# Wide products and compressed-block products cut into units of one weight tile and interleaved

## The chip, the cores and the metric

The kernel runs on one core of a Trainium2 chip. The metric is the device time of one execution in microseconds, here called us. Inside the core, PE (TensorE) multiplies matrices, PEld is its weight load, DVE (VectorE) and ACT (ScalarE) work element by element, POOL is GpSimd, and SP (SyncE) issues most of the transfers (DMAs).

## The reference

A decoder trunk of two layers over 1024 tokens of width 1024, in fp32. Layer A mixes tokens with a gated short convolution, layer B with sparse attention whose keys and values come in three kinds (compressed blocks, selected blocks, a sliding window). Both layers also attend to 256 memory tokens and end with a squared-ReLU MLP. What matters here, cut:

```python
for layer in range(2):
    h = rmsnorm(x, mix_norm[layer])
    mkv = mem_h @ mem_w_kv[layer]               # keys and values of the 256 memory tokens
    if layer == 0:
        z = h @ a_w_in[0]; y_tok = short_conv_mixer(z[..., :2304], a_conv_w[0])
    else:
        z = h @ b_w_in[0]                       # 768 queries, 36 gates, 256 memory queries
        y_tok = nsa_mixer(z[..., :768], z[..., 768:804], b_q_gain[0], *shared, rel_bias)
    y_mem = memory_attention(q_mem, mkv, ...)   # 4 heads
    x = x + concatenate([y_tok, y_mem]) @ w_out[layer]
    x = x + square(relu(rmsnorm(x, mlp_norm[layer]) @ w_up[layer])) @ w_down[layer]
    if layer == 0:
        kv = rmsnorm(x, kv_norm) @ w_kv_shared  # six parts of 128 columns
        # compress: overlapping blocks of 32 tokens, flattened to 2048, twice (keys, values)
        kc, vc = [gelu((blocks(kv, i) + cmp_pos[i]) @ cmp_w1[i]) @ cmp_w2[i] for i in (0, 1)]
        shared = (kc, vc, ks, vs, kw, vw)
```

## The kernel before

Tokens are worked in two chunks of 512 (c is 0 or 1). Every fp32 operand is split into a high and a low part (H and L), and a product is three matmuls: H with H, H with L, L with H (lines 265 to 267).

All weights are streamed from HBM in the order of a list called `plan`. An entry is a unit: a function and the weight tiles that it eats, each of at most 128x512 floats (256 KB). For a tile, `w_dma` (line 276) issues the load into `wraw` from SP; ACT writes its high part `wH` (line 261); DVE writes the low part `wL` (line 262). There are three buffers each of `wraw`, `wH` and `wL` (WB is 3), so a fourth load waits until the first tile's subtraction on DVE is done. `w_get` splits up to three tiles ahead and asks for two loads more.

Most units are dense: weights are stationary, 512 tokens are the moving columns, one output tile of 128 channels takes 24 matmuls and two weight tiles. Two other kinds stand among them:

- `wide`: tokens on partitions, weights as the moving operand, 8 k-steps into up to four PSUM banks (`mm,mm,lgb,lgb`). It makes the memory keys and values (`memkv_unit`, weights `mkv_w`, 512 columns, two banks), the keys and values of layer B (K, `kvt_w`, 512), the gates with the memory queries (M, `bm_w`, 292), and the queries in two groups of 384 (Q and q, `bq_w`). Each of these is one unit of 8 weight tiles. Its result goes through `heads`: copies and squares on ACT, sums on DVE, a power on POOL, transposes on PE (line 602), a scaled copy `hn` on ACT (line 606, one buffer) and a store (line 611).
- `cmp_unit`: the first product of the compression (line 1237, 256 columns, weights `cw1`, called cw in rows). One unit is two weight tiles with 8 matmuls, four units for the keys (c in ORDER) and four for the values (d) of each chunk.

ORDER (line 28) gives the sequence of these groups for each chunk, with u and U for the two dense units that feed the compression. P2 and P3 (lines 29 and 30) say how many dense units `weave` (line 1448) puts ahead of each group. The second layer's memory unit stands in `plan` after the convolution units of chunk 0 (line 1522), ahead of the output products. When a layer-B stage's groups are done, `attention` starts: its loads (ks, vs, kw, vw by POOL, T by SP) run beside the dense units that follow.

An issue planner with estimated costs lets evacuations run as threads beside the units; the recorded instructions are then ordered per engine, and loads may be put forward.

Of the kernel before, what the change touches and what calls it, by code (L numbers as in the profile page):

```python
# [24 lines left out]
S, D = 1024, 1024  # L25


ORDER = 'uUKccccMddddqQ', 'uUKccccMddddQq'
P2 = [0, 0, 1, 0, 5, 1, 2, 2, 2, 1, 1, 2, 0, 1]
P3 = [8, 0, 0, 0, 0, 1, 1, 0, 1, 0, 1, 1, 0, 4]  # L30
NTAIL = 6
AHEAD = 1
PACE = 2.5
# [4 lines left out]
KT = D // 128  # L38
# [25 lines left out]
class Issue:  # L64
# [30 lines left out]
    def spawn(self, gen):  # L95
        th = [gen, 0.0, False]
        self.threads.append(th)
        return th
# [32 lines left out]
def mmc(n):  # L131

    return (n if n >= 256 else 4 * n) / 2400
# [11 lines left out]
def trunk(ctx: ExitStack, tc: tile.TileContext, a, out):  # L145
# [11 lines left out]
    V, ACT, POOL, PE, DMA, LD = nc.vector, nc.scalar, nc.gpsimd, nc.tensor, nc.sync, nc.gpsimd  # L157
# [31 lines left out]
    qd = [[scratch(f"qd{c}_{t}", [128, 2, CH]) for t in range(6)] for c in range(2)]  # L189
# [14 lines left out]
    iss = Issue()  # L204
    chain, spawn = iss.chain, iss.spawn
# [140 lines left out]
    R, Hs = {}, {}  # L346
# [184 lines left out]

    FOUR = (mm, mm, lgb, lgb)

    def wide(hs, cols, evac, n, banks):

        kp = 512 // cols
        ps = []
        for b in banks:
            ps.append((yield from b.get())[:, :cols])
        for k in range(KT):  # L540
            if k % kp == 0:
                H, L = yield from w_get(n + k // kp, cols)
            yield lambda: len(hs) > k
            yield hs[k][2]
            for j in range(len(ps)):
                xH, xL = (x[:, 128 * j:128 * j + 128] for x in hs[k][:2])
                three(ps[j], xH, xL, H[:, k % kp], L[:, k % kp], k == 0, k == KT - 1)
                iss.pe(3 * mmc(cols))
                yield 0
        spawn(evac(ps, banks))  # L550

    def heads(ps, banks, nh, gains, dsts, dones, more=None, rkey=None):

# [58 lines left out]
            dones[i].t = max(t, t1) + 2.5  # L612
        raws.put(len(rw))

    def memkv_unit(l, dones, n):
        def evac(ps, banks):
            done = dones[2]

            def more(j):
                t = v_rows(ps[j][:, 256:], mvd[l][128 * j:128 * j + 128])  # L620
                done.t = t + 2.5
                return t
            yield from heads(ps, banks, 4, [nmkg[:, l:l + 1]] * 2, mkd[l], dones, more)
        yield from wide(Hs["mem"], 512, evac, n, (mm, lgb))


    def finish(pv, parts, dst, done):
# [422 lines left out]
            return free  # L1050
        yield from dense(n, Hs["a", c], evac)

    def qmem_wide(dones, n):
        yield from wide(Hs["a", 1], 256, lambda ps, banks: heads(
            ps, banks, 4, [mqg[:, 0:1]] * 2, mqd[0][1], dones, None, (0, 1)), n, FOUR)

    def first_units(*ns):

# [93 lines left out]
            return done.t  # L1152
        yield from dense(n, Hs["kv", c], evac)

    def kv_unit(c, dones, n):
# [9 lines left out]
        yield from wide(Hs["kv", c], 512, evac, n, FOUR)  # L1165

    def q_unit(c, i, dones, n):
        yield from wide(Hs["b", c], 384, lambda ps, banks: heads(
            ps, banks, 6, [qg] * 3, [qd[c][3 * i + t] for t in range(3)], dones), n, FOUR)

    def memgate_unit(c, dones, n):
# [15 lines left out]
        yield from wide(Hs["b", c], 292, evac, n, FOUR)  # L1187


    FS = {}  # L1190
# [31 lines left out]
    hid, through = {}, set()  # L1222

    def cmp_unit(kvi, c, j, flag, n):
        m = 64 + 2 * (31 + c)
        yield lambda: (kvi, c) in FS
        FT, t = FS[kvi, c]
        yield t
        if j == 0:
            hid[kvi, c] = yield from pvb.get()  # L1230
        ps = hid[kvi, c]
        for k in range(4):
            kk = 4 * j + k
            if k % 2 == 0:
                H, L = yield from w_get(n + k // 2, 256)
            for i, x in enumerate((H, L)):
                PE.matmul(ps[:m, :256], FT[kk // 8][:, kk % 8, :m], x[:, k % 2],
                          start=(kk == 0 and i == 0), stop=(kk == 15 and i == 1))
# [84 lines left out]
    def unit(lst, fn, *args, w=()):  # L1323
        lst.append((fn, args, w))
# [21 lines left out]
    def conv_units(m, c, t):  # L1346
        w = a["a_w"]
        unit(m, a_gate_c, c, t, w=[w[2 + 3 * t]])
        unit(m, a_u, c, t, w=[w[3 + 3 * t]])
        unit(m, a_gate_b, c, t, w=[w[4 + 3 * t]])  # L1350
# [44 lines left out]
                unit(m, down_unit, c, t, last, w=[a["wd"][l, b, t]])  # L1395
        return m

    def memkv_units(l, flags):
        m = []
        fl = [Flag(), Flag(), Flag()]  # L1400
        flags += fl
        unit(m, memkv_unit, l, fl, w=[(a["mkv_w"][l], 512)])
        return m

    normed = set()

    def b_norm(c):
# [6 lines left out]
    def kvb_units(c, flags):  # L1414
        m = []
        w = a["kv_w"]
        us = [Flag(), Flag()]

        def flag():
            flags.append(Flag())  # L1420
            return flags[-1]

        fl = [flag(), flag()]
        js = [0, 0]
        for ch in ORDER[c]:
            g = []
            if ch in "uU":
                i = "uU".index(ch)
                unit(g, u_unit, i, c, us[i], w=[w[i]])
                start(g, cmp_start, i, c, us[i])  # L1430
            elif ch == "K":
                unit(g, kv_unit, c, [flag(), flag(), flag()], w=[(a["kvt_w"], 512)])
            elif ch in "cd":
                i = "cd".index(ch)
                unit(g, cmp_unit, i, c, js[i], fl[i], w=[a["cw1"][i, js[i]]])
                js[i] += 1
            elif ch == "M":
                unit(g, memgate_unit, c, [flag(), flag(), flag()], w=[(a["bm_w"], 292)])
            else:
                i = "Qq".index(ch)  # L1440
                unit(g, q_unit, c, i, [flag(), flag(), flag()], w=[(a["bq_w"][i], 384)])
            m.append(g)
            if len(m) == 3:
# [57 lines left out]
    conv_units(plan, 0, 1)  # L1501
    plan += memkv_units(0, fmk[0])
    start(plan, mem_attn, 0, 0, fmq[0] + fmk[0], fy[0])
    for t in range(2, 6):
        conv_units(plan, 0, t)

    def after(n, box):

# [23 lines left out]
    plan += m[-8:]  # L1532


    unit(plan, qmem_wide, fmq[1], w=[(a["am_w"], 512)])
    start(plan, mem_attn, 0, 1, fmq[1] + fmk[0], fy[1])
    fkv, fat = {0: [], 1: []}, {0: [], 1: []}

# [166 lines left out]
```

## Time and profile before

| what | us |
|---|---|
| median of 3 runs | 2446.8 (2444.61 to 2448.54) |
| profiled execution, whole | 2446.22 |
| its span, first to last instruction | 2444.4 |
| PE busy | 2409.7 |
| DVE busy | 1509.3 |
| ACT busy | 1286.2 |

The granted clock over the span is 0.999. The profile names for each engine the time it was busy; for a gap it names the instruction that ended it. A matmul's record lasts longer than the distance at which the next may start, so busy PE time hides the short gaps: the distance from start to start shows them.

### The profile page before, as it was taken

How to read it: one execution, taken by the hardware profiler on the slowest of the kernel's cores; microseconds unless marked ns; L12 is line 12 of the kernel's file. 1: busy time of each engine (PE TensorE's matmuls, PEld its weight loads, DVE VectorE, ACT ScalarE, POOL GpSimd, SP SyncE). 2: the span in 40 equal slices, each digit the busy share in tenths (PEclk: the TensorE clock that was granted, in tenths of full speed). 3: DMA queues.
4: the chain of work that ended last, by engine and by line, in shares of the span. 5: the costliest groups of instructions: out<-in, count | busy, mean ns of one | idle time of the engine just before them, and what ended most of it. 6: DMA issues, size and time to landing. Idle time of an engine off the chain costs nothing.

```text
span 2444.4 us, 35761 instructions
## 1 busy us (share of the span) xinstructions
PE 2409.7 (99%) x12058; PEld 2028.1 (83%) x12058; DVE 1509.3 (62%) x3444; ACT 1286.2 (53%) x2719; POOL 234.6 (10%) x354
## 2 busy tenths in 40 slices
PE   8999999999999999999999999999999999999999
PEld 7878788888888888888888788888888888888887
DVE  7655344464757547777756764788878874644443
ACT  5544343354645537777754553677767763423332
POOL 1120000001100131111110012100010010000000
PEclk9999999999999999999999999999999999999999
DMA  6572553345554564353256557632263244333333
GB/s 183 152 210 93 180 167 97 121 136 164 155 161 142 156 183 129 106 135 104 84 174 200 175 169 203 149 94 74 72 141 87 79 150 137 103 96 98 96 97 106
DMA packets 206712, 327.26 MB, mean 134 GB/s; under 512 B 29763, under 2 KB 74501, under 8 KB 206144
## 3 DMA queue, kind: packets, MB, share of 16 engines
q1 hardware_dynamic: 179584, 287.97, 38.1%
q0 software_dynamic: 26944, 37.00, 7.1%
q8 instruction: 95, 1.56, 0.3%
q14 instruction: 89, 0.73, 0.1%
HBM read 282.63 MB, written 46.38 MB: 135 GB/s over the span
## 4 chain that ended last, share of the span: by engine, by line
PE 91%; DMA 4%; DVE 2%; ACT 1%; issue 1%; POOL 1%; SPq 0%; ACTq 0%; POOLq 0%; DVEq 0%
PE mm L265 24%; PE mm L267 24%; PE mm L266 24%; PE pv L902 5%; PE tr L886 4%; PE lg L802 2%; PE lg L803 2%; PE lg L265 1%; PE lg L267 1%; PE lg L266 1%; DVE wL L262 1%; DMA wraw<-in_mkv_w_dram 1%; DMA mv<-ev 1%; PE lg L699 1%; PE pv L735 1%
## 5 line engine op out<-in xcount | busy, mean ns | idle before, releaser
L261 ACT ACTIVATE wH<-wraw 128x512 fp32r<-128x512 f32 (+2 forms) x776 | 480.9, 621 | 767.5 <-PE mm L266 574.0
L262 DVE TENSOR_TENSOR wL<-wraw,wH 128x512 fp32r<-128x512 f32 (+2 forms) x776 | 526.4, 680 | 432.9 <-ACT wH L261 424.1
L265 PE MATMUL mm<-pH,wH 128*128 128x512 f32 x1448 | 574.8, 397 | 9.2 <-ACT wH L261 9.2
L267 PE MATMUL mm<-pH,wL 128*128 128x512 f32 x1448 | 566.4, 391 | 0.4 <-DVE wL L262 0.4
L266 PE MATMUL mm<-pL,wH 128*128 128x512 f32 x1448 | 566.1, 391 | 0.5 <-DMA pL<-yd 0.3
L265 PE MATMUL mm<-qH,wH 128*128 128x512 f32 x1152 | 458.4, 398 | 2.6 <-ACT wH L261 2.6
L267 PE MATMUL mm<-qH,wL 128*128 128x512 f32 x1152 | 450.2, 391 | 1.6 <-DVE wL L262 1.4
L266 PE MATMUL mm<-qL,wH 128*128 128x512 f32 x1152 | 449.5, 390 | 0.0
L265 PEld LDWEIGHTS mm<-pH,wH 128*128 128x128 f32 x1448 | 272.7, 188 | 63.4 <-ACT wH L261 11.6
L267 PEld LDWEIGHTS mm<-pH,wL 128*128 128x128 f32 x1448 | 272.4, 188 | 59.9 <-DVE wL L262 2.3
L266 PEld LDWEIGHTS mm<-pL,wH 128*128 128x128 f32 x1448 | 273.0, 189 | 51.8 <-DMA pL<-yd 0.7
L267 PEld LDWEIGHTS mm<-qH,wL 128*128 128x128 f32 x1152 | 216.2, 188 | 50.6 <-DVE wL L262 4.5
L265 PEld LDWEIGHTS mm<-qH,wH 128*128 128x128 f32 x1152 | 216.6, 188 | 47.8 <-ACT wH L261 4.9
L266 PEld LDWEIGHTS mm<-qL,wH 128*128 128x128 f32 x1152 | 216.7, 188 | 38.6
L262 DVE TENSOR_TENSOR ptL<-tr,ptH 128x512 fp32r<-128x512 f32 (+3 forms) x284 | 175.1, 628 | 45.1 <-ACT ptH L261 43.0
L261 ACT ACTIVATE ptH<-tr 128x512 fp32r<-128x512 f32 (+3 forms) x284 | 150.7, 544 | 63.3 <-PE tr L886 55.9
L1138 DVE TENSOR_TENSOR x<-mm,x 128x512 f32<-128x512 f32 x128 | 88.2, 689 | 129.7 <-PE mm L267 129.6
L643 POOL TENSOR_TENSOR mv<-ev,mv 64x128 f32<-64x128 f32 (+1 forms) x128 | 76.2, 595 | 694.7 <-DMA mv<-ev 358.0
L262 DVE TENSOR_TENSOR qL<-relu,qH 128x512 fp32r<-128x512 f32 x128 | 88.4, 691 | 84.4 <-ACT qH L261 84.0
L814 ACT ACTIVATE ss<-ss,st 128x32 f32<-128x32 f32 (+1 forms) x192 | 105.5, 550 | 44.4 <-DVE st L808 42.4
L261 ACT ACTIVATE qH<-relu 128x512 fp32r<-128x512 f32 x128 | 80.5, 629 | 34.9 <-DVE relu L1124 33.4
L886 PE MATMUL tr<-ident,ss 128*128 128x128 f32 (+2 forms) x528 | 81.9, 274 | 0.1
(249 smaller groups left out, 3288.8 us busy)
## 6 DMA issues: line engine op xcount, KB each, us to landing
wraw<-in_wu_dram SPq DMA_DIRECT2D x256, 256.0 KB
wraw<-in_wd_dram SPq DMA_DIRECT2D x256, 256.0 KB
wraw<-in_a_w_dram SPq DMA_DIRECT2D x76, 256.0 KB
wraw<-in_wo_dram SPq DMA_DIRECT2D x64, 256.0 KB
yd<-yo SPq DMA_DIRECT2D x80, 128.0 KB
skd<-rvd SPq DMA_DIRECT2D x12, 703.0 KB
sw<-xsd SPq DMA_DIRECT2D x32, 256.0 KB
wraw<-in_cw_dram SPq DMA_DIRECT2D x32, 256.0 KB
```

The source lines that it names most:

```text
L261: ACT.activation(H, src, AF.Copy)
L262: V.tensor_tensor(L, src, f(H), op=OP.subtract)
L265: PE.matmul(ps, wH, xH, start=start, stop=False)
L266: PE.matmul(ps, wH, xL, start=False, stop=False)
L267: PE.matmul(ps, wL, xH, start=False, stop=stop)
L643: POOL.tensor_tensor(mv[lo:lo + 64, :w], ev[lo:lo + 64, c0:c1], mv[lo:lo + 64, :w], op=OP.add)
L802: PE.matmul(lg[:, :p1 - p0], lhs, kh[:, base + p0:base + p1], start=True, stop=False)
L803: PE.matmul(lg[:, :p1 - p0], lhs, kl[:, base + p0:base + p1], start=False, stop=True)
L814: ACT.activation(x[:, x0:x1], x[:, x0:x1], AF.Exp, bias=nm[:, hf, br, n:n + 1], scale=-1.0, accum_out=l_[:, hf, br:br + 1])
L886: PE.transpose(tr[:w, 256 * j + 128 * hf:256 * j + 128 * hf + 128], x[hf][:, o:o + w], ident)
L902: PE.matmul(pv[:, :256], v, x[:w, 256 * j:256 * j + 256], start=(gi == 1 and j == 0 and k == 0), stop=(new is None and j == len(ks) - 1 an ...
L1138: V.tensor_tensor(x, ps, x, op=OP.add)
```

## The change

`wide` becomes `wide_units`: one unit for each weight tile, with the PSUM banks taken in the first and the evacuation started by the last. `cmp_unit` eats one tile instead of two. The smaller units are then interleaved by `mixed`, one from each list in turn:

- the second layer's memory tiles, one after each of the last six convolution units of chunk 0, and two more behind them; before, all eight stood in a row after these units;
- M's eight tiles with the eight of the key compression (before: two compression tiles at a time between dense units, then M as a block);
- the last query group's eight tiles with the eight of the value compression (before: again pairs between dense units, then both query groups).

ORDER loses c and d; P2 and P3 get six gaps in place of fourteen. The start of layer B's scaling thread moves to the K group. Matmuls, tiles, bytes and the work of ACT and DVE are the same in number.

```diff
-ORDER = 'uUKccccMddddqQ', 'uUKccccMddddQq'
-P2 = [0, 0, 1, 0, 5, 1, 2, 2, 2, 1, 1, 2, 0, 1]
-P3 = [8, 0, 0, 0, 0, 1, 1, 0, 1, 0, 1, 1, 0, 4]
+ORDER = 'uUKMqQ', 'uUKMQq'
+P2 = [0, 0, 1, 5, 5, 4]
+P3 = [8, 0, 0, 3, 3, 3]
...
-    def wide(hs, cols, evac, n, banks):
+    def wide_units(m, key, cols, evac, w, banks=FOUR):
...
         kp = 512 // cols
-        ps = []
-        for b in banks:
-            ps.append((yield from b.get())[:, :cols])
-        for k in range(KT):
-            if k % kp == 0:
-                H, L = yield from w_get(n + k // kp, cols)
...
+        hs, ps = Hs[key], []
+
+        def piece(k0, n):
+            if k0 == 0:
+                for b in banks:
+                    ps.append((yield from b.get())[:, :cols])
+            H, L = yield from w_get(n, cols)
+            for k in range(k0, k0 + kp):
...
+            if k0 + kp == KT:
+                spawn(evac(ps, banks))
+
+        for k0 in range(0, KT, kp):
+            unit(m, piece, k0, w=[(w[:, k0 * cols:(k0 + kp) * cols], kp * cols)])
...
     def cmp_unit(kvi, c, j, flag, n):
...
-        for k in range(4):
-            kk = 4 * j + k
-            if k % 2 == 0:
-                H, L = yield from w_get(n + k // 2, 256)
+        H, L = yield from w_get(n, 256)
+        for k in range(2):
+            kk = 2 * j + k
...
-        if j == 3:
+        if j == 7:
...
+        def cmp_units(i):
+            m, fl = [], flag()
+            for j in range(8):
+                unit(m, cmp_unit, i, c, j, fl, w=[a["cw1"][i, j // 2][:, 512 * (j % 2):512 * (j % 2) + 512]])
+            return m
...
+            elif ch == "M":
+                memgate_units(g, c, flags3())
+                g = mixed(g, cmp_units(0))
+            else:
+                q_units(g, c, "Qq".index(ch), flags3())
+                if ch == ORDER[c][-1]:
+                    g = mixed(g, cmp_units(1))
+            m.append(g)
         return m
+
+    def mixed(xs, ys):
+
+        return [u for pair in zip(xs, ys) for u in pair]
...
-    for t in range(2, 6):
+    for t in range(2, 4):
         conv_units(plan, 0, t)
+    m = []
+    for t in range(4, 6):
+        conv_units(m, 0, t)
+    kv = memkv_units(1, fmk[1])
+    plan += mixed(m, kv) + kv[len(m):]
...
-    plan += memkv_units(1, fmk[1])
     plan += out_units(0, 0, x_here)
```

The order of the loads on SP shows the three places. At the second layer's memory product, the rows before run from the last convolution tile (a_w) into the memory tiles (mkv); `mv` and `yd` belong to the first memory attention, `ss<-in_xT` are tokens loaded for the output products:

```order
L276 DMA wraw<-in_a_w_dram 128x512
L276 DMA wraw<-in_mkv_w_dram 128x512
L649 DMA yd_0_7_113<-yo 128x1x256
L961 DMA ss<-in_xT_dram 128x512 x2
L637 DMA mv<-ev 64x256
L276 DMA wraw<-in_mkv_w_dram 128x512
L961 DMA ss<-in_xT_dram 128x512 x2
L637 DMA mv<-ev 64x256
```

After the change, the memory tiles stand among the convolution tiles:

```order
L277 DMA wraw<-in_mkv_w_dram 128x512
L277 DMA wraw<-in_a_w_dram 128x512 x2
L277 DMA wraw<-in_mkv_w_dram 128x512
L649 DMA mv<-ev 64x256
L277 DMA wraw<-in_a_w_dram 128x512 x2
L649 DMA mv<-ev 64x256
L661 DMA yd_0_6_112<-yo 128x1x256
L277 DMA wraw<-in_mkv_w_dram 128x512
L649 DMA mv<-ev 64x256
L277 DMA wraw<-in_a_w_dram 128x512
L661 DMA yd_0_6_112<-yo 128x1x256
L277 DMA wraw<-in_a_w_dram 128x512
```

Each memory load now follows one or two convolution loads, and the `in_xT` loads come behind. At the gates of chunk 0 (bm is M, cw the compression, wu a dense unit's tiles, kcd and kd stores of keys), before:

```order
L276 DMA wraw<-in_bm_w_dram 128x292 x3
L1250 DMA w_7980<-in_cw_dram 128x128
L276 DMA wraw<-in_bm_w_dram 128x292 x4
L1308 DMA kcd<-kco 64x2x31 x2
L276 DMA wraw<-in_bm_w_dram 128x292
L276 DMA wraw<-in_wu_dram 128x512 x4
L276 DMA wraw<-in_cw_dram 128x512 x2
L276 DMA wraw<-in_wu_dram 128x512 x2
L276 DMA wraw<-in_cw_dram 128x512
```

And after:

```order
L277 DMA wraw<-in_bm_w_dram 128x292
L619 DMA kd_158<-hn 256x1x512
L277 DMA wraw<-in_cw_dram 128x512
L996 DMA sw<-xsd_7_97 128x512
L619 DMA kd_159<-hn 256x1x512
L277 DMA wraw<-in_bm_w_dram 128x292
L277 DMA wraw<-in_cw_dram 128x512
L277 DMA wraw<-in_bm_w_dram 128x292
L277 DMA wraw<-in_cw_dram 128x512
L277 DMA wraw<-in_bm_w_dram 128x292
L277 DMA wraw<-in_cw_dram 128x512
```

Blocks of M tiles, and pairs of cw tiles beside dense ones, become strict alternation with no dense tile between. At the last query group of chunk 0 (bq is Q and q, wd a dense unit's tiles, qd the stores of the first group's queries, vcd of compressed values), before:

```order
L276 DMA wraw<-in_cw_dram 128x512 x2
L276 DMA wraw<-in_bq_w_dram 128x384 x8
L276 DMA wraw<-in_wd_dram 128x512 x2
L276 DMA wraw<-in_bq_w_dram 128x384 x5
L1317 DMA vcd<-vco 31x128 x2
L276 DMA wraw<-in_bq_w_dram 128x384 x3
```

And after:

```order
L277 DMA wraw<-in_bq_w_dram 128x384
L277 DMA wraw<-in_cw_dram 128x512
L619 DMA qd_3_141<-hn 128x1024
L277 DMA wraw<-in_bq_w_dram 128x384
L619 DMA qd_4_142<-hn 128x1024
L277 DMA wraw<-in_cw_dram 128x512
L277 DMA wraw<-in_bq_w_dram 128x384
L619 DMA qd_5_143<-hn 128x1024
L277 DMA wraw<-in_cw_dram 128x512
L277 DMA wraw<-in_bq_w_dram 128x384
L277 DMA wraw<-in_cw_dram 128x512
```

Sixteen query tiles in a row, with cw pairs ahead of them, become one query group alone (ahead of these rows) and one that alternates with cw, with the first group's three stores among the loads.

## Rows read from the trace of the kernel before

**Rows 1.** The page, part 1: busy time of each engine

```profile
PE 2409.7 (99%) x12058; PEld 2028.1 (83%) x12058; DVE 1509.3 (62%) x3444; ACT 1286.2 (53%) x2719; POOL 234.6 (10%) x354
```

**Rows 2.** PE's waits in the whole span: total, times, longest, in us

```profile
PE mm L265 <- ACT wH L261: 14.1, 11, 6.5
...
PE tr L1299 <- POOL r L1294: 1.2, 1, 1.2
PE tr L602 <- DVE raw L587: 1.2, 1, 1.2
```

**Rows 3.** Stretches: length; busy PE, PEld, DVE, ACT, POOL; clock; DMA share, GB/s

```profile
146.00:166.00 20.00, 15.56 (x54) 10.55 (x54) 11.32 (x18) 8.79 (x17) 3.12 (x5) 0.91 0.81 245
727.00:925.00 198.00, 191.51 (x980) 163.65 (x979) 117.76 (x217) 96.74 (x193) 32.98 (x38) 1.00 0.55 163
887.00:925.00 38.00, 34.53 (x158) 27.34 (x158) 18.87 (x35) 13.69 (x25) 5.93 (x4) 1.00 0.59 195
1386.00:1537.00 151.00, 146.76 (x763) 126.61 (x762) 91.14 (x176) 73.01 (x151) 31.57 (x37) 0.99 0.67 194
```

**Rows 4.** PE's timeline (start, us, what) where each memory layer's product begins and ends

```profile
57.49 0.39 PE L265 MATMUL mm<-wH,memH 128*128 128x512 f32 x1
...
68.48 0.39 PE L265 MATMUL mm<-pH,wH 128*128 128x512 f32 x1
...
146.92 0.50 PE L265 MATMUL mm<-wH,memH 128*128 128x512 f32 x1
...
165.73 0.39 PE L265 MATMUL mm<-qH,wH 128*128 128x512 f32 x1
```

**Rows 5.** Timelines of PE around the first and the last of 68 gaps

```profile
728.62 0.28 PE L1237 MATMUL pv<-wL,FT 128*126 128x256 f32 x1
729.10 0.50 PE L265 MATMUL mm<-qH,wH 128*128 128x512 f32 x1 [0.20 <-ACT wH L261]
...
1520.09 0.40 PE L267 MATMUL mm<-qH,wL 128*128 128x512 f32 x1
1520.42 0.33 PE L602 MATMUL tr<-ident,raw 128*128 128x128 f32 x1
```

**Rows 6.** Timelines: a weight tile's issue on SP, its split on ACT and DVE

```profile
60.48 0.33 SPq L276 DMA_DIRECT2D wraw<-in_mkv_w_dram  x1
...
63.43 0.63 ACT L261 ACTIVATE wH<-wraw 128x512 fp32r<-128x512 f32 x1 [0.90 <-DMA wraw<-in_mkv_w_dram]
...
64.09 0.69 DVE L262 TENSOR_TENSOR wL<-wraw,wH 128x512 fp32r<-128x512 f32 x1 [0.84 <-ACT wH L261]
...
844.03 0.33 SPq L276 DMA_DIRECT2D wraw<-in_bq_w_dram  x1
...
846.53 0.52 ACT L261 ACTIVATE wH<-wraw 128x384 fp32r<-128x384 f32 x1
```

**Rows 7.** PE's timeline: two neighbouring products each of 292, 256 and 384 columns

```profile
793.06 0.30 PE L266 MATMUL mm<-wL,sh 128*128 128x292 f32 x1
793.19 0.30 PE L267 MATMUL mm<-wH,sh 128*128 128x292 f32 x1
...
844.86 0.28 PE L1237 MATMUL pv<-wH,FT 128*126 128x256 f32 x1
844.98 0.28 PE L1237 MATMUL pv<-wL,FT 128*126 128x256 f32 x1
...
848.06 0.33 PE L266 MATMUL lg<-wL,sh 128*128 128x384 f32 x1
848.24 0.33 PE L267 MATMUL lg<-wH,sh 128*128 128x384 f32 x1
```

**Rows 8.** Timelines of ACT and SP while the attention's loads run

```profile
890.38 0.69 ACT L606 ACTIVATE hn<-tr,qg 128x512 fp32r<-128x512 f32 x1 [6.31 <-DMA qd<-hn]
...
1498.70 0.33 SPq L276 DMA_DIRECT2D wraw<-in_wd_dram  x1
...
1509.08 0.63 ACT L261 ACTIVATE wH<-wraw 128x512 fp32r<-128x512 f32 x1 [2.69 <-DMA wraw<-in_wd_dram]
```

More of the change, by code (lines that the diff above doesn't have):

```diff
@@ L532, in trunk @@
     FOUR = (mm, mm, lgb, lgb)
-    def wide(hs, cols, evac, n, banks):
+    def wide_units(m, key, cols, evac, w, banks=FOUR):
         kp = 512 // cols
-        ps = []
-        for b in banks:
-            ps.append((yield from b.get())[:, :cols])
-        for k in range(KT):
-            if k % kp == 0:
-                H, L = yield from w_get(n + k // kp, cols)
[L543 to L550, printed above, removed]
+        hs, ps = Hs[key], []
[5 more added lines that the diff above has]
+            for k in range(k0, k0 + kp):
+                yield lambda: len(hs) > k
+                yield hs[k][2]
+                for j in range(len(ps)):
+                    xH, xL = (x[:, 128 * j:128 * j + 128] for x in hs[k][:2])
+                    three(ps[j], xH, xL, H[:, k % kp], L[:, k % kp], k == 0, k == KT - 1)
+                    iss.pe(3 * mmc(cols))
+                    yield 0
+            if k0 + kp == KT:
+                spawn(evac(ps, banks))
+        for k0 in range(0, KT, kp):
+            unit(m, piece, k0, w=[(w[:, k0 * cols:(k0 + kp) * cols], kp * cols)])
     def heads(ps, banks, nh, gains, dsts, dones, more=None, rkey=None):
@@ L613, in heads, with memkv_units @@
         raws.put(len(rw))
-    def memkv_unit(l, dones, n):
+    def memkv_units(l, flags):
+        m = []
+        dones = [Flag(), Flag(), Flag()]
+        flags += dones
         def evac(ps, banks):
-            done = dones[2]
             def more(j):
                 t = v_rows(ps[j][:, 256:], mvd[l][128 * j:128 * j + 128])
-                done.t = t + 2.5
+                dones[2].t = t + 2.5
                 return t
             yield from heads(ps, banks, 4, [nmkg[:, l:l + 1]] * 2, mkd[l], dones, more)
-        yield from wide(Hs["mem"], 512, evac, n, (mm, lgb))
+        wide_units(m, "mem", 512, evac, a["mkv_w"][l], (mm, lgb))
+        return m
     def finish(pv, parts, dst, done):
@@ L1051, in a_gate_b, with qmem_wide @@
         yield from dense(n, Hs["a", c], evac)
-    def qmem_wide(dones, n):
-        yield from wide(Hs["a", 1], 256, lambda ps, banks: heads(
-            ps, banks, 4, [mqg[:, 0:1]] * 2, mqd[0][1], dones, None, (0, 1)), n, FOUR)
+    def qmem_wide(m, dones):
+        wide_units(m, ("a", 1), 256, lambda ps, banks: heads(
+            ps, banks, 4, [mqg[:, 0:1]] * 2, mqd[0][1], dones, None, (0, 1)), a["am_w"])
     def first_units(*ns):
@@ L1153, in u_unit, with kv_units @@
         yield from dense(n, Hs["kv", c], evac)
-    def kv_unit(c, dones, n):
+    def kv_units(m, c, dones):
         def evac(ps, banks):
@@ L1164, in evac, with q_units, memgate_units @@
                              [kd[b][:, :, CH * c:CH * c + CH] for b in range(2)], dones, more)
[L1165 to L1171, printed above, removed]
+        wide_units(m, ("kv", c), 512, evac, a["kvt_w"])
+    def q_units(m, c, i, dones):
+        wide_units(m, ("b", c), 384, lambda ps, banks: heads(
+            ps, banks, 6, [qg] * 3, [qd[c][3 * i + t] for t in range(3)], dones), a["bq_w"][i])
+    def memgate_units(m, c, dones):
         def evac(ps, banks):
@@ L1186, in evac @@
                              more, (1, c))
-        yield from wide(Hs["b", c], 292, evac, n, FOUR)
+        wide_units(m, ("b", c), 292, evac, a["bm_w"])
     FS = {}
@@ L1231, in cmp_unit @@
         ps = hid[kvi, c]
-        for k in range(4):
-            kk = 4 * j + k
-            if k % 2 == 0:
-                H, L = yield from w_get(n + k // 2, 256)
+        H, L = yield from w_get(n, 256)
+        for k in range(2):
+            kk = 2 * j + k
             for i, x in enumerate((H, L)):
-                PE.matmul(ps[:m, :256], FT[kk // 8][:, kk % 8, :m], x[:, k % 2],
+                PE.matmul(ps[:m, :256], FT[kk // 8][:, kk % 8, :m], x[:, k],
                           start=(kk == 0 and i == 0), stop=(kk == 15 and i == 1))
@@ L1396, in mlp_units @@
         return m
[L1398 to L1403, printed above, removed]
     normed = set()
@@ L1421, in flag, with flags3 @@
             return flags[-1]
-        fl = [flag(), flag()]
-        js = [0, 0]
+        def cmp_units(i):
+            m, fl = [], flag()
+            for j in range(8):
+                unit(m, cmp_unit, i, c, j, fl, w=[a["cw1"][i, j // 2][:, 512 * (j % 2):512 * (j % 2) + 512]])
+            return m
+        def flags3():
+            return [flag(), flag(), flag()]
         for ch in ORDER[c]:
@@ L1431, in kvb_units @@
             elif ch == "K":
[L1432 to L1443, printed above, removed]
+                kv_units(g, c, flags3())
                 do(g, lambda: spawn(x_scale(("b", c), reload(lambda k: xsd[c][k]), ("b", c), C_MIXG + 8,
                                             s_tiles(), pace=PACE)))
-        return m
+            elif ch == "M":
[6 more added lines that the diff above has]
+            m.append(g)
+        return m
+    def mixed(xs, ys):
+        return [u for pair in zip(xs, ys) for u in pair]
     def weave(m, groups, gaps):
@@ L1503, in trunk @@
     start(plan, mem_attn, 0, 0, fmq[0] + fmk[0], fy[0])
-    for t in range(2, 6):
+    for t in range(2, 4):
         conv_units(plan, 0, t)
+    m = []
+    for t in range(4, 6):
+        conv_units(m, 0, t)
+    kv = memkv_units(1, fmk[1])
+    plan += mixed(m, kv) + kv[len(m):]
     def after(n, box):
@@ L1532, in trunk @@
     plan += m[-8:]
-    unit(plan, qmem_wide, fmq[1], w=[(a["am_w"], 512)])
+    qmem_wide(plan, fmq[1])
     start(plan, mem_attn, 0, 1, fmq[1] + fmk[0], fy[1])
```

## The prediction

> **What bounds the kernel now.** I read the page's busy times first: PE is busy 99% of the span, DVE 62%, ACT 53% [rows 1]. The change adds no matmul and takes none away, so only what PE does not use can move: gaps. The second view is what PE waits for. The longest entry is weights, 14.1 us in 11 waits for `wH` from ACT; two single waits of 1.2 us are for transposes [rows 2]. The third view, stretches of the trace, says where. The second layer's memory product is the one plain hole: of 20 us from 146, PE is busy 15.56, at a granted clock of 0.91. In the layer-B stage of chunk 0 (727 to 925) PE is idle 6.5 of 198 us, in that of chunk 1 (1386 to 1537) 4.2 of 151 [rows 3]. Idle time understates it. A record of 512 columns lasts 0.39 us, while in layer 0's memory product 48 of them take 10.99 us, 0.23 each [rows 4], so each gap hides up to 0.16. I therefore measured from start to start. The first such gap, after a pair of compression tiles, has 0.48 us between starts where 0.12 is usual; the last, before a transpose, has 0.33 in place of 0.23 [rows 5, 7]. There are 68 gaps of 0.1 us or more over the usual in these two stages, 28 and 40, and they sum to 10.2 and 10.1: **20.3 us**.
>
> What the gaps have in common is the weight stream. PE's need for a tile depends on the product: a memory tile is 6 matmuls of 512 columns, 10.99/8 = 1.37 us [rows 4]; a dense tile is 12, 2.74; an M tile 12 x 0.133 = 1.6 us; a Q tile 12 x 0.175 = 2.1 us; a compression tile 4 x 0.12 = 0.48 us [rows 7]. Against it stands what the three buffers can deliver. In a calm stretch, a 256 KB load is issued at 60.48, ACT begins on it at 63.43, DVE ends at 64.09 + 0.69, and only then is the buffer's next load issued. A lap is 4.3 us for three tiles: 1.43 us for one. A 384-column tile needs 2.5 us to ACT and, with its ACT time of 0.52 in place of 0.63, about 1.1 for the split: 3.6 us [rows 6]. For 292 columns I take the same 2.5 and 0.95 for the split, 3.45. So any tile below 1.43 us of PE time makes PE wait for its successor, unless tiles in hand cover it. When the loads of the attention run at the same time, delivery is far worse: a load issued at 1498.70 is met by ACT at 1509.08, 10.4 us later, and at 890.38 ACT has stood 6.31 us before `hn`, which waits for a store of queries [rows 8].
>
> **The change part by part.**
>
> (1) Memory tiles between convolution units. Layer 0's product, with the same eight tiles, takes 68.48 - 57.49 = 10.99 us; layer 1's takes 165.73 - 146.92 = 18.81 [rows 4]. The hole is 7.8 us: loads issued late and beside token loads, and ACT waiting. Interleaved, one unit of two dense tiles and a memory tile need 2 x 2.74 + 1.37 = 6.85 us of PE for three tiles, where a calm lap is 4.3: 2.5 us of delay on every load are covered. The two memory tiles left at the end have the dense output products behind them and can lose about 1 us. The token loads come after, beside dense tiles, where three take 8.2 us for a lap of 4.3. The bounds are 0 left and the old 7.8 left; I take 1.0, since six of eight tiles are covered: **-6.8**.
>
> (2) M with the key compression, no dense tile between. A pair needs 1.6 + 0.48 = 2.08 us, 1.04 for a tile. Its mean lap is (3.45 + 4.3)/2 = 3.9, or 1.29 for a tile. The deficit is 0.25 x 16 tiles = 4.0 us, less about 1.2 that the three tiles in hand at the start cover: 3 us in calm, and 2.7 more for each half microsecond by which loads come late. Before, M's tiles alone had 1.6 us against 1.15, and a pair of compression tiles had dense ones about it. In these stretches loads move at 163 to 194 GB/s on average [rows 3], so I take a quarter microsecond of delay: **4.5 in each chunk, 9.0**. Bounds: 3, and 8 at a full microsecond.
>
> (3) The last query group with the value compression. A pair needs 2.1 + 0.48, 1.28 for a tile; the mean lap is 3.95, or 1.32. In calm the deficit is 0.04 x 16 = 0.6 us, covered by what is in hand: nothing. Now the attention's loads decide. They start once the memory keys and K are through, which the change leaves where it was, ahead of the last query tiles; before, these tiles came as plain Q tiles, 2.1 us of PE for a lap of 3.6, and so bore 2.7 us of delay; the wait showed only behind them, 38 us with 3.5 idle from 887 [rows 3]. Now the alternation stands in that place and has no slack. With d us of delay the deficit is (3.95 + d)/3 - 1.28 a tile, times 16, less 2 in hand. I take d as 1.1 for chunk 0 and 1.4 for chunk 1, whose stretch moves more (194 against 163 GB/s): 4.4 and 6.0, **10.4**. Bounds: 0 with no delay; with 2.5 us, a fourth of the 10.4-us case, 12 each.
>
> The Trainium skill, "DMA: Bandwidth & Descriptors", section "Queues, rings and completion order", says that each DMA engine goes round the queue rows for which it has work, packet by packet: weights issued by SP would share the engines with POOL's loads and get no precedence. By that rule delay d follows the load on all queues, which speaks against this part; the 10.4 us from issue to split agree, and a full sharing would give the case below with 12 us in each chunk.
>
> (4) What stays of the old gaps. Dense tiles behind the mixes can absorb late loads, so of the old gaps behind the last query group I leave 2.0. The two waits for a transpose [rows 2] and the gaps behind them come from the order of `heads`, which now changes: half stays, 2.5 of some 5.
>
> (5) Nothing else is priced. Units of one tile cost PE no instruction; the scaling thread's start moves by no more than the dense units ahead of it. If their cover is gone, ACT and DVE (busy 73 and 91 of 151 us in chunk 1 [rows 3]) would show it as waits for `sh`.
>
> Stages: 9.0 + 10.4 + 2.0 + 2.5 = 23.9 against 20.3: +3.6. With -6.8 the sum is **-3.2**. The profiled run took 2446.2, 0.6 below the median of 2446.8, so the forecast is 2446.8 - 3.2 = 2443.6, with rounding and a little for unpriced work **2444**.
>
> **Rivals.**
>
> The ring keeps up. If the interleaving spreads demand and load delay stays near nothing, M costs 3 each, the last group 0, the tail 2 and the transposes 2.5: 10.5 against 20.3, with -6.8 a gain of 16.6, less 1 for unpriced work: **2431**. For it speaks that the compression pairs, each of which cost its gap behind, are gone from beside dense tiles, and that a pair of Q and cw needs almost what a calm lap gives. Against it: the loads of the attention are in the same place. The Trainium skill, "Perfetto Trace Analysis", section "Optimization Strategy", says that interleaving regimes with different most-contended engines may improve performance; the rows agree only for part (1), where a dense regime with slack is mixed in. In (2) and (3) both members are poor in slack, and by that rule alone this rival's 2431 would come out.
>
> The attention's loads starve the alternation (**the slower side**). Place: the last query group in both chunks. Mechanism: SP's weight loads queue behind or beside POOL's, and each lap grows; ACT, holding `hn` for the earlier stores, cannot split. At 2.5 us of delay there and a full microsecond in M the stages cost 2 x 12 + 2 x 8 + 4.5 = 44.5, +24.2, with -6.8 it is +17.4: **2464**. It decides once the delay in the last group passes about 1.9 us: 0.75 us above mine costs 16/3 x 0.75 = 4 us in each chunk. For it: 10.4 us in one load, and 6.31 us of ACT [rows 8]. Against: those are single loads at the peak.
>
> The change does less than it says: tiles are interleaved but the loads bunch, since they may be put forward. The order on SP speaks against it: loads alternate as units do. Then (1) would keep most of its 7.8 and the rest stay: **2447**.
>
> **How the numbers follow.** My sum holds within about 7 us either way (2437 to 2451) and gets 0.42; the ring that keeps up 0.28; starvation 0.22; the change without effect 0.08. Of my own case 0.12 falls under 2441.9, 0.28 lies within 0.2% of the median (4.9 us, about what a measurement of this kernel can tell from no change) and 0.02 above 2451.7. Faster is then 0.28 + 0.12 = 0.40; same 0.28 + 0.08 = 0.36; slower 0.22 + 0.02 = 0.24. For 8 in 10 the range reaches to 2429 below and 2461 above, leaving out the far half of either rival. By itself, the likeliest case spans 2437 to 2451.
>
> **What would show it.** (1): the eight memory products stand apart, each with no gap over 0.3 us, and the clock row near 146 shows 1.00. (2): in each M mix, starts 3 to 5 us late in all, spread as short gaps of some 0.3 us at each pair, with `wH` or `wL` as what ended them. (3): the same in the last group, growing from its middle, where POOL's loads land; issue to split 3.5 to 4.5 us against 2.95. (4): the two 1.2-us waits for transposes gone or moved. I am wrong if the mixes have no gaps (the lap is shorter than three buffers suggest), if one load in the last group takes over 8 us, or if the time moves outside these stretches, in the attention of either chunk.

## The result, and the profile after

The changed kernel takes 2474.1 us (median of 4 runs, 2470.84 to 2474.28), the kernel before 2447.15 beside it. The ratio is 1.0106, 95% interval 1.0094 to 1.0118: **27 us slower**. The forecast was 2444, with a range to 2461. The result lies beyond the starved rival's 2464.

The page of the changed kernel, part 1, and its longest waits of PE (total, times, longest in us; all line numbers are one or more higher than before):

```profile
PE 2419.7 (98%) x12058; PEld 2038.9 (82%) x12058; DVE 1509.5 (61%) x3444; ACT 1290.6 (52%) x2719; POOL 231.9 (9%) x354
```

```profile
PE mm L266 <- ACT wH L262: 22.1, 12, 6.4
PE pv L1249 <- ACT wH L262: 8.1, 5, 3.3
PE lg L814 <- DVE st L820: 6.7, 5, 3.1
```

In the first fence DVE and ACT are as busy as before [rows 1]. In the second, wide and dense products (`mm`) wait 22.1 us for `wH` where they waited 14.1 [rows 2]. The compression's own products (`pv L1249`) wait 8.1; in the kernel before, where their line is 1237, it was:

```profile
PE pv L1237 <- ACT wH L261: 0.2, 1, 0.2
```

The third line of the second fence belongs to the attentions of both chunks. PE's busy time itself is 10 us longer for the same 12058 matmuls; part of that is a lower clock, of which more below. The stretches (length; busy PE, PEld, DVE, ACT, POOL; granted clock; DMA share; GB/s) show where:

```profile
109.00:158.00 49.00, 47.98 (x238) 39.49 (x236) 32.63 (x69) 25.87 (x59) 13.98 (x21) 1.00 0.69 200
749.80:773.00 23.20, 19.67 (x133) 17.61 (x131) 14.75 (x27) 13.49 (x33) 0.00 (x0) 0.99 0.47 141
845.00:878.00 33.00, 26.14 (x139) 24.01 (x139) 12.05 (x22) 13.56 (x27) 9.12 (x15) 0.95 1.04 227
878.00:925.00 47.00, 45.93 (x232) 37.92 (x231) 31.19 (x74) 22.95 (x54) 8.00 (x8) 1.00 0.51 155
925.00:1340.00 415.00, 410.82 (x2147) 345.95 (x2146) 276.70 (x805) 269.75 (x693) 55.68 (x97) 1.00 0.46 129
1413.00:1440.00 27.00, 22.50 (x141) 20.22 (x140) 17.64 (x33) 15.79 (x38) 0.00 (x0) 0.94 0.56 172
1492.00:1529.00 37.00, 27.20 (x139) 24.64 (x138) 11.46 (x19) 12.23 (x23) 7.68 (x13) 0.86 0.96 225
1529.00:1570.00 41.00, 38.27 (x180) 30.93 (x179) 22.22 (x49) 14.40 (x32) 7.96 (x7) 0.96 0.55 167
```

In order: the interleaved memory tiles; in chunk 0 the alternation of M with key compression, that of the last query group with value compression, what follows, and the attention; in chunk 1 the two alternations and what follows. As before, I counted gaps of 0.1 us or more over the usual distance from start to start on PE's timeline, since idle time hides up to 0.16 us of each:

| stretch | before | after |
|---|---|---|
| memory tiles and the convolution units around them | 9.1 | 3.6 |
| M alternations, chunk 0 and 1 | in the stages | 6.0 + 8.1 |
| last query group alternations | in the stages | 10.1 + 14.8 |
| behind them | in the stages | 1.7 + 4.8 |
| layer-B stages in all | 20.7 | 47.8 |
| attention of chunk 0 | 4.5 | 10.4 |

That is -5.5, +27.1 and +5.9, together 27.5 us, about the difference of the two spans, 28.1. Everything lies in the stretches that the prediction named, but for the attention. (The attention has many short products. With the usual distance taken for each shape by itself its row is 1.9 and 7.3; the difference is nearly the same.) Each trace is one execution, and the runs of one kernel spread by 3 to 12 us, so two such counts that differ by 2 or 3 us may be equal.

The lap of the buffers can be read from the timelines of SP and ACT. First a calm load in the first M alternation, then the longest in the second query alternation:

```profile
753.84 0.33 SPq L277 DMA_DIRECT2D wraw<-in_bm_w_dram  x1
...
756.80 0.43 ACT L262 ACTIVATE wH<-wraw 128x292 fp32r<-128x292 f32 x1
...
1514.16 0.33 SPq L277 DMA_DIRECT2D wraw<-in_bq_w_dram  x1
...
1523.41 0.52 ACT L262 ACTIVATE wH<-wraw 128x384 fp32r<-128x384 f32 x1 [4.62 <-DMA wraw<-in_bq_w_dram]
```

From issue to split 2.96 us in one place, 9.25 in the other. Over the last 14 of the 16 loads each, the query alternations have a mean of 5.2 us in chunk 0 and 6.1 in chunk 1, the M alternations 3.3 and 3.8; the calm rows say 2.5 to 2.95 [rows 6]. In the query alternations the loads turn slow where POOL begins to issue those of the attention, in chunk 0 and in chunk 1 at:

```profile
850.89 4.70 POOL L684 DMA_DIRECT2D ks<-mkd  x8 [20.34 <-issue]
...
1498.11 4.70 POOL L684 DMA_DIRECT2D ks<-mkd  x8 [14.83 <-issue]
```

The last four weight loads issued before the first of these took 2.6 to 3.8 us to their split, the eight behind it 4.6 to 8.0; in chunk 1 the last three before took 2.5 to 3.9, the eight behind 4.5 to 9.3.

### The profile page after: what moved, and what is told of

It is laid out like the page before. It is cut to its first block, busy times and chain, and to the rows that moved or that the text cites. A ratio compares the mean times of both kernels' runs of the same rounds, so it can differ in the third digit from the quotient of the medians.

```text
span 2472.5 us, 35763 instructions
## 1 busy us (share of the span) xinstructions
PE 2419.7 (98%) x12058; PEld 2038.9 (82%) x12058; DVE 1509.5 (61%) x3444; ACT 1290.6 (52%) x2719; POOL 231.9 (9%) x354
## 4 chain that ended last, share of the span: by engine, by line
PE 88%; DMA 5%; DVE 3%; ACT 2%; issue 1%; POOL 1%; SPq 0%; ACTq 0%; POOLq 0%; DVEq 0%
PE mm L266 24%; PE mm L268 24%; PE mm L267 24%; PE pv L914 4%; PE tr L898 4%; PE lg L814 2%; PE lg L815 2%; DMA wraw<-in_cw_dram 2%; DMA mv<-ev 1%; DMA wraw<-in_bq_w_dram 1%; DVE wL L263 1%; PE lg L266 1%; PE lg L267 1%; PE lg L268 1%; ACT wH L262 1%
## 5 line engine op out<-in xcount | busy, mean ns | idle before, releaser
L262 ACT ACTIVATE wH<-wraw 128x512 fp32r<-128x512 f32 (+1 forms) x776 | 480.8, 621 | 764.4 <-PE mm L267 587.6
L263 DVE TENSOR_TENSOR wL<-wraw,wH 128x512 fp32r<-128x512 f32 (+1 forms) x776 | 526.4, 680 | 445.7 <-ACT wH L262 439.1
```

The lines of the kernel that those rows point to most:

```text
L262: ACT.activation(H, src, AF.Copy)
L263: V.tensor_tensor(L, src, f(H), op=OP.subtract)
```

## The experiments

Two theories of the loss. **Starved**: the alternation of queries with compression is fed well enough by three buffers alone, and it is the attention's loads, in the same place, that delay the weights. **Too thin**: two products with little PE time for each tile follow one another, and three buffers cannot feed that even alone. The first three runs separate the three parts, the others the causes. In the first run all tiles are cut into units of their own too; from 180 us on, behind its memory tiles, the traces show PE's and SP's instructions in the same order as in the kernel before. So in the layer-B stages the cutting alone does nothing, and only places matter.

**Memory tiles alone.** ORDER, P2 and P3 as before, with c and d as two one-tile units each; only this differs from the kernel before:

```diff
+    kv = memkv_units(1, fmk[1])
+    plan += mixed(m, kv) + kv[len(m):]
...
-    plan += memkv_units(1, fmk[1])
```

> Only the second layer's memory tiles are interleaved with convolution units; the compression pairs, M and the query groups stand where they stood in the kernel before. Both theories: the hole of 8 us at the memory product shrinks to about 3, nothing else moves: 2442 us, 5 below the kernel before.

Measured: 2442.0 us against 2446.2, ratio 0.9985 (0.9976 to 0.9995). As expected: this part is worth 4 us.

**M alternating with key compression alone**, at M's old place (X in ORDER is M mixed with c):

```diff
-ORDER = 'uUKccccMddddqQ', 'uUKccccMddddQq'
+ORDER = 'uUKXddddqQ', 'uUKXddddQq'
+P2 = [0, 0, 1, 10, 2, 1, 1, 2, 0, 1]
+P3 = [8, 0, 0, 2, 1, 0, 1, 1, 0, 4]
```

> Only M and the key compression alternate, at the place where M stood; everything else as in the kernel before. Both theories: the two alternations lose 6 and 8 us as in the changed kernel, the key pairs' gaps of about 5 go: 2456 us, 9 above the kernel before. Under 2450 would say that the loss in the changed kernel comes from where its alternation stands.

Measured: 2456.4, ratio 1.0041 (1.0026 to 1.0055), 10 us slower. The two alternations, columns as above:

```profile
778.00:803.00 25.00, 23.60 (x151) 21.03 (x150) 12.06 (x22) 13.33 (x33) 0.00 (x0) 1.00 0.43 131
1396.00:1427.00 31.00, 26.06 (x159) 22.20 (x158) 24.13 (x43) 18.23 (x42) 0.77 (x1) 1.00 0.60 182
```

PE is idle 1.4 and 4.9 us in them, and they lose 3.8 and 8.5 us from start to start.

**Last query group alternating with value compression alone**, with 18 and 17 dense units ahead of the attention as before (Y and y are Q and q mixed with d):

```diff
-ORDER = 'uUKccccMddddqQ', 'uUKccccMddddQq'
+ORDER = 'uUKccccMqY', 'uUKccccMQy'
+P2 = [0, 0, 1, 0, 5, 1, 2, 2, 6, 1]
+P3 = [8, 0, 0, 0, 0, 1, 1, 0, 3, 4]
```

> Only the last query group and the value compression alternate, with the same number of dense units ahead as in the kernel before. Both theories: 10 and 15 us lost in the two alternations, about 4 of pair gaps and some 5 of the old gaps behind the group gone: 2462 us, 15 above the kernel before. If the attention of chunk 0 also costs 7 us more, as in the changed kernel, the cause is the alternation; if not, it is the smaller number of dense units ahead of it.

Measured: 2468.9, ratio 1.0094 (1.0073 to 1.0114), 23 us slower and 7 more than expected. The two alternations, columns as above:

```profile
862.00:899.00 37.00, 29.79 (x146) 25.32 (x145) 15.55 (x28) 14.56 (x28) 12.18 (x18) 0.90 1.02 236
1487.00:1524.00 37.00, 28.50 (x136) 26.30 (x135) 10.53 (x18) 10.88 (x22) 7.68 (x13) 0.82 0.97 210
```

PE is idle 7.2 and 8.5 us of 37 and loses 13.7 and 14.4 from start to start. The attention of chunk 0 has no extra gaps here. So most of the change's cost is in this one part.

**Loads behind the alternation.** The changed kernel, with the attention's first loads tied to the last product of the last query group: ACT writes one column of each of their tiles from that product, before POOL may load over it.

```diff
+                if j == 0:
...
+                    for t in [k[:, 0, 256 * h:256 * h + 1] for h in range(4)] + [v[:, 0, :1], qs[0][:, 0, :1], qs[1][:, 0, :1], w[:, 0, :1], vw[:, 0, :1]]:
+                        ACT.activation(t, ps[0][:, :1], AF.Copy)
+                    held[c] = k, v, qs, w, vw
```

> The changed kernel, but the attention's first loads (ks, vs, qs, kw, vw) are tied by a one-column write to the last product of the last query group, so that they run behind the alternation. Starved by these loads: the alternation's loss falls from 25 us to under 6, issue to split there under 3.6 us on average, and the time falls to about 2455. Too thin in itself (three buffers cannot feed the alternation even alone): the loss stays over 15 us and the time within 6 us of 2474.

Measured: 2468.5, ratio 1.0098 (1.0074 to 1.0121): by the medians some 5 us less than the changed kernel, not the 19 expected, and the intervals of the two ratios overlap. The stretches show two things at once, the alternation and what follows it, for chunk 0 and then chunk 1:

```profile
844.00:868.00 24.00, 23.89 (x141) 22.65 (x140) 11.46 (x20) 13.37 (x34) 1.80 (x3) 1.00 0.63 194
868.00:925.00 57.00, 46.92 (x221) 38.15 (x220) 30.13 (x71) 22.83 (x53) 15.52 (x21) 0.91 0.73 172
1490.00:1514.00 24.00, 23.71 (x141) 22.30 (x140) 11.27 (x18) 11.96 (x31) 1.45 (x3) 1.00 0.63 212
1514.00:1570.00 56.00, 45.96 (x216) 37.51 (x215) 29.19 (x69) 20.98 (x50) 15.81 (x21) 0.91 0.95 200
```

The alternations are whole: PE is idle 0.1 and 0.3 us, and loses 0.9 and 1.3 from start to start in place of 10.1 and 14.8; issue to split is 3.4 and 3.6 us on average. That settles the theories for this part: three buffers feed this alternation, and the loads starve it. But the loss is only moved: behind it PE is now idle 10 us in each chunk. From start to start, the alternations and what follows them lose 29.7 us in all, in the changed kernel 31.4. The wait of PE and, on ACT's timeline, what stood behind it:

```profile
PE tr L610 <- DVE hn L615: 7.9, 1, 7.9
```

```profile
890.96 0.69 ACT L614 ACTIVATE hn<-tr,qg 128x512 fp32r<-128x512 f32 x1 [8.60 <-DMA vcd<-vco]
```

The transposes of the last queries waited 7.9 us for `hn`, for which ACT had waited 8.6 us, in the end on the store of the compressed values (`vcd<-vco`, issued at 880.0): the burst now meets the stores of the last group. In both places the burst met something that needed DMA soon, and had its price.

**Value compression with the first query group.** As the third run, but the group that alternates is the first, and the last is plain:

```diff
-ORDER = 'uUKccccMqY', 'uUKccccMQy'
+ORDER = 'uUKccccMyQ', 'uUKccccMYq'
```

> Like the run in which only queries and value compression alternate (2469 us), with one difference: the value compression alternates with the first query group, and the last group stands alone. If the attention's loads are what starves the alternation, they now run beside the plain query group as before the change, the alternation loses under 2 us in each chunk, and the time is 2443 to 2448. If an alternation of queries and compression is too thin anywhere, 20 us stay lost: about 2466.

Measured: 2450.1, ratio 1.0009 (0.9999 to 1.0019): 19 us less than the third run, though 2 above the interval named. The stretches are, for each chunk, the alternation and what follows it:

```profile
839.00:866.00 27.00, 24.93 (x140) 24.05 (x139) 10.95 (x20) 11.63 (x24) 1.86 (x3) 0.94 0.59 157
866.00:930.00 64.00, 62.89 (x321) 54.10 (x320) 35.80 (x79) 25.19 (x55) 20.13 (x23) 1.00 0.74 194
1437.00:1466.00 29.00, 26.99 (x149) 25.78 (x148) 13.04 (x23) 13.78 (x28) 1.96 (x4) 0.94 0.65 169
1466.00:1545.00 79.00, 76.14 (x368) 63.34 (x368) 39.52 (x77) 28.20 (x56) 18.61 (x21) 1.00 0.73 193
```

The alternation loses 3.8 and 3.7 us, not 14; the plain last group bears the burst at a DMA share of 0.74 with PE idle 1.1 of 64 us. A calm lap would give no loss; mean issue to split is 4.0 and 4.3 us, so some delay remains there, and what causes it is open.

**M's alternation with dense units in it.** As the second run, with one dense unit behind every pair (None stands for it, and `weave` fills it in):

```diff
-P2 = [0, 0, 1, 10, 2, 1, 1, 2, 0, 1]
-P3 = [8, 0, 0, 2, 1, 0, 1, 1, 0, 4]
+P2 = [0, 0, 1, 2, 2, 1, 1, 2, 0, 1]
+P3 = [8, 0, 0, 0, 0, 0, 0, 1, 0, 4]
...
-                    g = mixed(g, cmp_units(0))
+                    g = [u for p in zip(g, cmp_units(0), [None] * 8) for u in p]
```

> Like the run in which only M and the key compression alternate (2456 us), but a dense unit stands behind every pair, so that four tiles need 7.5 us of PE, 1.9 each, against a calm lap of 1.3. If three buffers cannot deliver an alternation that needs 1.04 us a tile: the loss of some 14 us in the two alternations falls under 4 and the time to 2444 to 2449. If the loss came from something else in M's place (the scaling thread that makes its operands, DVE's load), it stays near 2456.

Measured: 2455.6, ratio 1.0038 (1.0028 to 1.0049): a miss in the time. The stretches are chunk 0's alternation, then in chunk 1 its first 14 us and the rest; below them PE's waits in those 14 us:

```profile
737.00:799.00 62.00, 60.60 (x330) 52.59 (x330) 42.73 (x72) 33.81 (x69) 1.01 (x1) 1.00 0.46 145
1386.00:1400.00 14.00, 8.39 (x36) 6.53 (x35) 9.86 (x21) 6.89 (x19) 4.11 (x2) 0.76 0.50 163
1400.00:1453.00 53.00, 53.00 (x283) 46.23 (x283) 33.01 (x55) 27.67 (x56) 0.00 (x0) 1.00 0.48 148
```

```profile
PE tr L610 <- DVE raw L595: 3.5, 1, 3.5
PE mm L266 <- ACT sh L262: 1.8, 1, 1.8
```

In chunk 0 the loss is 1.7, of which 1.4 is a wait for something else (the residual `x` from DVE); in chunk 1 it is nothing from 1400 on. But in chunk 1 I had put M right behind K, two dense units earlier, so that its operands `sh` and K's own evacuation came too late: 8.4 us. My sequence, not the theory, lost there.

**The same, two dense units later in chunk 1**, with a dense unit behind every second pair there:

```diff
-P3 = [8, 0, 0, 0, 0, 0, 0, 1, 0, 4]
+P3 = [8, 0, 0, 2, 0, 0, 1, 1, 0, 1]
...
-                    g = [u for p in zip(g, cmp_units(0), [None] * 8) for u in p]
+                    xs = [None] * 8 if c == 0 else [[], None] * 4
+                    g = [u for p in zip(g, cmp_units(0), xs) for u in p if u != []]
```

> The run with a dense unit behind each pair of M and key compression again (2456 us), but in chunk 1 the alternation begins two dense units later, as in the run with the bare alternation, so that M's operands are ready, with a dense unit behind every second pair. If the missed 9 us were M starting before its operands in chunk 1: the 8 us of gaps at its start go, the alternation loses under 3 us in each chunk, and the time is 2445 to 2451. If dense units between the pairs don't help: 2454 to 2458.

Measured: 2450.8, ratio 1.0027 (1.0018 to 1.0037). The alternations, then PE's longest wait behind them:

```profile
737.00:799.00 62.00, 60.71 (x331) 52.65 (x330) 42.80 (x74) 34.06 (x69) 1.01 (x1) 1.00 0.44 145
1396.00:1435.00 39.00, 38.54 (x226) 33.95 (x224) 31.83 (x54) 25.45 (x56) 0.00 (x0) 1.00 0.58 185
```

```profile
PE mm L266 <- ACT wH L262: 6.2, 2, 4.3
```

They lose 1.6 and 1.5 us in place of 3.8 and 8.5: M's alternation is too thin for the laps that it gets, and dense tiles between the pairs cure its gaps. The time does not show it as clearly: it is still 6 us above the kernel before, and the interval overlaps that of the bare alternation. Of the 6.2 us of waits that stay, 4.3 lie behind the last query group, where only one dense unit now stands between the two groups; P3 had four. Whether that distance is the cause was not tried. The other 2.0 lie ahead of the first query group, behind the pairs of value tiles.

**The changed kernel with 18 dense units** ahead of the attention of chunk 0:

```diff
-P2 = [0, 0, 1, 5, 5, 4]
+P2 = [0, 0, 1, 5, 8, 4]
```

> The changed kernel with 8 in place of 5 dense units ahead of the first query group of chunk 0, so that the attention starts behind 18 dense units as in the kernel before (15 in the changed one). If the attention's 7 us of extra gaps in chunk 0 come from that shift: 2467 to 2470. If they come from the alternation: 2472 to 2477.

Measured: 2462.6, ratio 1.0067 (1.0047 to 1.0086), 11 us less than the changed kernel and below the 2467 to 2470 expected. The attention of chunk 0, in the changed kernel's stretch above with 4.2 us idle, in the kernel before, and here:

```profile
925.00:1330.00 405.00, 405.00 (x2148) 342.50 (x2147) 282.87 (x830) 274.71 (x716) 58.64 (x100) 1.00 0.47 132
```

```profile
925.00:1345.00 420.00, 419.51 (x2214) 354.35 (x2213) 291.06 (x844) 282.87 (x726) 58.56 (x100) 1.00 0.47 132
```

PE is idle 0 and 0.5 us, and the gaps are 5.1 us against 10.4. So the attention's extra gaps came from starting three dense units earlier; by which of its loads is not followed up. The other 5 us came off in chunk 1 (its M alternation 5.3 for 8.1, its tail 2.4 for 4.8), which I did not expect and have not explained. It also means that the parts do not add up exactly: alone they give -4, +10 and +23, a sum of 29, and all three at the same distance give 16.

**Two versions for a better kernel.** The memory tiles with the alternation in the first query group (the first and the fifth run together):

```diff
-ORDER = 'uUKMqQ', 'uUKMQq'
-P2 = [0, 0, 1, 5, 5, 4]
-P3 = [8, 0, 0, 3, 3, 3]
+ORDER = 'uUKccccMyQ', 'uUKccccMYq'
+P2 = [0, 0, 1, 0, 5, 1, 2, 2, 6, 1]
+P3 = [8, 0, 0, 0, 0, 1, 1, 0, 3, 4]
```

> The memory interleave (4.2 us below the kernel before) together with the alternation of compression and first query group, all else as in the kernel before. If loads in the last group are the cause: 2439 to 2444, below both kernels. If not: about 2462.

Measured: 2445.7, ratio 0.9996 (0.9985 to 1.0006), above the 2444 named: 4 below the fifth run, as the memory part says, but 1 below the kernel before where the memory tiles alone are 4 below. By the medians, even at the better place this alternation loses more than the old pairs; the intervals overlap. The other version adds to the memory tiles single compression tiles in chunk 0, one to a dense unit (there c and d are one tile each):

```diff
+ORDER = 'uUKccccccccMddddddddqQ', 'uUKccccMddddQq'
+P2 = [0, 0, 1, 0, 1, 1, 1, 1, 1, 1, 1, 1, 1, 1, 1, 1, 1, 1, 1, 1, 0, 1]
+P3 = [8, 0, 0, 0, 0, 1, 1, 0, 1, 0, 1, 1, 0, 4]
```

> The memory interleave (2442 us alone), and in chunk 0 sixteen single compression tiles with one dense unit between each in place of eight pairs. A tile and a dense unit need 5.9 us of PE for three loads, 2 us each, against a calm lap of 1.43 each. If a compression tile costs PE only where two or more follow one another: the pairs' gaps of some 3 us in chunk 0 go and the time is 2437 to 2441. If singles wait as pairs do: 2441 to 2445.

Measured: 2436.6 against 2444.6, ratio 0.9970 (0.9959 to 0.9980), below both kernels. The same work, from K's end to the last query tiles of chunk 0, in the kernel before and here:

```profile
727.00:846.00 119.00, 115.97 (x590) 96.86 (x589) 80.86 (x143) 68.26 (x137) 13.29 (x16) 1.00 0.49 153
```

```profile
722.50:838.00 115.50, 114.93 (x591) 97.17 (x590) 80.61 (x143) 69.39 (x139) 12.36 (x16) 1.00 0.50 160
```

PE is idle 0.6 in place of 3.0 us, and the gaps fall from 5.4 to 1.6. None of the gaps that are left stands beside a compression product (`pv`): such a tile costs PE no gap of 0.1 us or more when a dense unit stands on either side.

## Why the prediction was wrong

**The bound and most of the places were right.** PE's gaps moved, and they moved in the stretches named, but for 6 us in the attention of chunk 0. That was among the prediction's signs of being wrong, as was a load of over 8 us in the last group (9.25). From -3.2 to the 28 us by which the span grew is 31 us: 14.5 of them are part (3), 6 the attention, 5 part (2). With (3) right and the rest as said, the forecast would have been some 2458, still within its range.

**(1) Memory tiles.** -6.8 was said; the run alone gave -4.2, the gaps 5.5. The hole closed as said (1.0 us idle of 49 in place of 4.4 of 20 [rows 3], and the clock at 1.00 for 0.91). I had left 1 us for what stays; 3.6 stay, of which 1.7 lie behind the last three memory tiles, which stand in a row, and 1.9 in the memory attention, whose products had 1.1 before.

**(2) M's alternation.** 9.0 was said, 14.1 came, 12.3 alone. The mechanism was right: the cure of its gaps by dense tiles shows that it is the lap. The formula held too: with the means measured in the same trace, 3.3 and 3.8 us from issue to split against a calm 2.7, the delay is 0.6 and 1.1, and it gives 6.2 and 8.8, against 6.0 and 8.1. The delay that I put in, a quarter microsecond, was too small: the loads ahead of the alternation came late (5.1 and 6.2 us for the second M tile and the compression tile behind it), and in chunk 1 nine of the 14 took 3.4 us or more. What delays them in chunk 1 is open.

**(3) The last query group. This is the step that failed.** 10.4 was said, 24.9 came. The formula holds: with the means measured in the same trace, 5.2 and 6.1 us, the delay d is 2.5 and 3.4, and (3.95 + d)/3 - 1.28, times 16, less 2 gives 11.9 and 16.7, against 10.1 and 14.8 measured. That is a check of the ring alone, since a measured lap holds every reason for which a tile came late; that the reason is the attention's loads, the fourth run shows. What failed is d. I took 1.1 and 1.4 from the average traffic of the whole stages (163 and 194 GB/s [rows 3]), although the same paragraph says that the attention's loads fall into just this stretch. There, the DMA share is 1.04 and 0.96 at 227 and 225 GB/s. The price stood in a row that I had set aside as a single load at the peak: 10.4 us from issue to split [rows 8]. My bound of 12 each was nearly the value. The starved rival, with 0.22, was the right one in the first of its two mechanisms. The second, ACT held by `hn`, hardly occurs. ACT's waits in the alternation of chunk 0, then of chunk 1 (us in all, times, longest):

```profile
ACT wH L262 <- DMA wraw<-in_cw_dram: 10.3, 4, 5.7
ACT wH L262 <- DMA wraw<-in_bq_w_dram: 4.4, 2, 2.5
...
ACT hn L614 <- DMA qd<-hn: 0.5, 1, 0.5
```

```profile
ACT wH L262 <- DMA wraw<-in_bq_w_dram: 12.4, 5, 4.6
ACT wH L262 <- DMA wraw<-in_cw_dram: 8.1, 4, 4.0
...
ACT hn L614 <- DMA qd<-hn: 2.0, 2, 1.8
```

The rule of the Trainium skill, "DMA: Bandwidth & Descriptors", section "Queues, rings and completion order", that a DMA engine goes round the queue rows packet by packet, agrees with this: SP's loads were slow beside POOL's, and the delay left the alternation when POOL's loads did (3.4 us). That it is this arbitration, and not the sum of bytes, no run here shows.

**(4) What stays.** 2.0 and 2.5 were said; behind the groups 6.5 stayed, most of it in chunk 1.

**(5) Nothing else priced.** Two things were missed. The attention of chunk 0 began three dense units earlier and lost 6 us; the sums of P2, 18 and 15, were there to be read. And long gaps cost clock. On PE's timeline behind the longest gap of the last alternation:

```profile
1519.91 0.27 PE L1249 MATMUL pv<-wL,FT 128*128 128x256 f32 x1
1523.99 0.69 PE L266 MATMUL mm<-wH,sh 128*128 128x384 f32 x1 [3.81 <-ACT wH L262]
...
1525.39 0.52 PE L266 MATMUL mm<-wH,sh 128*128 128x384 f32 x1
1525.71 0.52 PE L267 MATMUL mm<-wL,sh 128*128 128x384 f32 x1
```

Products of 384 columns start every 0.32 us, where 0.175 is usual [rows 7]. The granted clock of that alternation is 0.86, so part of the time ran at 1.2 in place of 2.4 GHz; counted by such distances, 28 products in the two query alternations lost 0.10 to 0.15 us each, 3.8 us in all, which is inside the 24.9.

The rule of the Trainium skill on interleaving regimes ("Perfetto Trace Analysis", section "Optimization Strategy") held as far as the rows had said: it paid where one member had slack (memory tiles or single compression tiles among dense ones), and not where neither had (M or the last queries with compression tiles).

## What to carry to other kernels

When a stream of loads feeds the engine that is the bound, work out for every product how long it keeps the engine per tile, and put the short ones singly among long ones, not among other short ones. Price the delay of a load from the stretch in which the load will run, with the other traffic that runs there, and not from a stage's average; when a burst of other loads cannot be avoided, lay it beside work that has slack for its loads (here the plain query group), and away from stores that someone waits for.

## What the runs showed of the hardware

A long gap of PE is paid twice. Behind 3.8 us without work, products started at half the usual rate, and in the two query alternations the granted clock was 0.95 and 0.86, with 10.1 and 14.8 us of gaps in them; with the same alternations alone it was 0.90 and 0.82. In the same place without the gaps (the run with the loads behind the alternation) it was 1.00. Not every gap does it: where M alternates in the changed kernel, the clock was 0.99 with 6.0 us of gaps in chunk 0 and 0.94 with 8.1 in chunk 1, and 1.00 with 8.5 where it alternates alone.

And moving a burst of loads behind the alternation did not remove its price: there PE was idle 10 us in each chunk, where it had been idle 7 and 10 within the alternation. Laid beside the plain query group, the burst left PE idle for 1.1 of 64 us in chunk 0 and 2.9 of 79 in chunk 1.
